# The FFN output projections as seven quarter products by tokens

## The chip, the cores and the metric

The kernel runs on one core of a Trainium2 chip. TensorE (PE) multiplies matrices, VectorE (DVE), ScalarE (ACT) and GpSimd (POOL) do elementwise work, and SyncE (SP) issues most transfers between HBM and the on-chip memory SBUF. PE's results land in PSUM, in eight banks of 128 partitions x 512 float32. Each engine works through its own instructions in order and waits for the others by semaphores. The metric is the device time of one execution in microseconds, as the median of several runs.

## The reference

A decoder trunk of two layers over 512 tokens and 1024 features, all in float32. Each layer has a token mixer (retention in layer 0, a gated linear recurrence, LRU, in layer 1) and a feed-forward network (FFN):

```python
def swiglu_ffn(x, w_in, w_out):
    gate, up = jnp.split(x @ w_in, 2, axis=-1)
    return (jax.nn.silu(gate) * up) @ w_out

# in the loop over the layers, behind the mixer:
    f = swiglu_ffn(rms_norm(x, norm_g[layer, 2]), ffn_w_in[layer], ffn_w_out[layer])
    x = x + rms_norm(f, norm_g[layer, 3])
```

The hidden width is 2816, which is 22 tiles of 128. The change concerns the last product, `h @ w_out` (512 x 2816 by 2816 x 1024), its norm over the 1024 features of each token, and the addition to `x`, once in each layer.

## The kernel before

**Precision.** A float32 value is split into a high part (`hi`, a cast to fp32r by ACT) and a low part (`lo`, the difference, by DVE), and a product is three matmuls (`mm3`, lines 289 to 291): high by high, high by low and low by high. So each weight chunk of 128 x 1024 costs one cast on ACT (L170) and one subtraction on DVE (L172) before PE can use it.

**Order.** One program writes all engines' instructions. A virtual clock, moved on by the columns of each matmul, decides what is written when: `later.after(ns, f)` puts `f` behind `ns` more of matmul time, `later.until` writes waiting work until something is there. Engines then follow that written order. Weight chunks are handled by `advance`: while one is used, the next ones are split up to `LEAD_S` = 12000 ns ahead, at most `HELD` = 8 at once, and their loads are issued ahead of that by SP. Memory for chunks, parts and intermediates comes from 50 slots of 128 x 1024.

**The FFN's input projection** already works by seven products of quarters in place of eight (a Strassen scheme in Winograd's form), pair of feature tiles by pair: products `p1` to `p7` with the weight forms `b11`, `t1`, `b21`, `t2`, `b22`, `t3`, `t4`, where `t1` to `t4` are sums of quarters made by accumulating loads (`Form.add`, L195, POOL's queue adds from HBM into the chunk). The activations are the stationary operand (128x128, loaded by LDWEIGHTS), the weight forms stream by 512 columns. There are five pairs per layer; `turn` (L999) transposes the gated result by four 128x128 transposes into one bank, and ACT copies it to the tiles `hf` of `h`, features on the partitions (L1000).

**The output projection** (`out_proj` with `quick=True`) is the plain product. Its stationary operand is the weight (`wh_fo`, `wl_fo`), and `h` streams: `halve` (L1145, L1146) splits `hf` into `hh` and `hl`. The 1024 features go in four groups of two tiles of 128, with 22 x 2 x 3 matmuls each: groups 0 to 2 with all 512 tokens (396 matmuls of 512 columns), the last one by two halves of 256 tokens (264 of 256). `tile_done` squares each tile (L616), scales it by the gain (L618) and adds the squares (L617); `finish` then sums the squares over the partitions by matmuls with ones (`st_`, L384), takes the root (`rchain`, L362 to L373), spreads it over partitions by two 128x128 matmuls (`rb_`, L398), multiplies (L624), adds the residual (L628, DVE and POOL) and stores (L629). In layer 0, `finish` of the second half lies in the LRU's first matmuls (`ps_u`, `ps_y`), and also writes the LRU's input tiles `Xl`; in layer 1 it is the end of the program.

Of the kernel before, what the change touches and what calls it, by code (L numbers as in the profile page):

```python
# [115 lines left out]
def trunk(ctx: ExitStack, tc: tile.TileContext, t: dict):  # L116
# [58 lines left out]
    class Form(Item):  # L175
# [326 lines left out]

    def product(key, r, banks, first, pre, done=None):

        for e in range(2):
            with Chunk("s", *key, WEIGHTS[r], e) as w:
                for p in range(2):
                    for i in range(2):
                        x = pre.left(LEFT[r], 2 * e + i, p)
                        mm3(banks[p], x, [z[:, i * S:(i + 1) * S] for z in w], first and not e + i, e + i == 2, True)  # L510
                    if e and done:
                        done(p)
# [86 lines left out]
    def out_proj(name, K, H, gi, x_src, pre, out, joined=1, halved=1, quick=False):  # L599
# [57 lines left out]
        for a, b in HALVES:  # L657
# [42 lines left out]
    def plan_ffn(layer):  # L700
# [287 lines left out]
    def ffn(layer, pre, x_src, nxt, out, mid=None):  # L988


        H, HF = [None] * KF, []
        A, B, C = ([acc(f"{z}{layer}_{p}") for p in range(2)] for z in "abc")
        def turn(hs, put):

            for m in range(hs[0].shape[-1] // 256):
# [43 lines left out]
        def closed(half):  # L1039
# [32 lines left out]
        def pair(j, r, to):  # L1072
# [4 lines left out]
            def gated():  # L1077
                hs, g = kept["u"], kept["g0"]
                for p in range(2):
                    dve.scalar_tensor_tensor(out=hs[p], in0=hs[p], scalar=pre.cols[p], in1=g[p], op0=ALU.mult, op1=ALU.mult)  # L1080
                later.after(W_TURN, lambda: turn(hs, lambda m: to[m][:, :, :256]))

# [33 lines left out]
            elif r == "p4":  # L1116
# [25 lines left out]

        def halve(n):
            f, hi, lo = HF[n], slot(f"hh{layer}_{n}", F32R), slot(f"hl{layer}_{n}", F32R)
            act.copy(hi, f)  # L1145
            dve.tensor_tensor(lo, f, hi.bitcast(F32), op=ALU.subtract)  # L1146
            for m in range(2):
                H[2 * n + m] = hi[:, m * S:(m + 1) * S], lo[:, m * S:(m + 1) * S]

# [4 lines left out]
        for j in range(PAIRS):  # L1154
            for r in LATER_PAIR if j else FIRST_PAIR[2:]:
# [223 lines left out]
```

## Time and profile before

| | us |
|---|---|
| median of 3 runs (lowest, highest) | 1355.41 (1354.25, 1356.55) |
| the profiled execution | 1356.11 |
| its span from first to last instruction | 1354.3 |
| PE busy | 1324.1 |
| PE's weight loads busy | 1122.6 |
| DVE busy | 826.6 |
| ACT busy | 712.3 |
| POOL busy | 135.7 |

The span begins at 0 in all rows. PE's busy time counts matmuls whose ends are modelled: a 512-wide one lasts 0.39 us in the rows, and the next one begins 0.23 us after it began, so lengths of a stretch are read from starts. The granted clock of PE was 0.996 of full speed over the span.

### The profile page before, as it was taken

What the parts mean: (1) busy time and instruction counts of PE and PEld (TensorE: products, weight loads), DVE (VectorE), ACT (ScalarE), POOL (GpSimd) and SP (SyncE); (2) the same over time, 40 slices, a digit from 0 to 9 for tenths busy, and PEclk for the clock granted to TensorE, in tenths of its full rate; (3) what the DMA queues carried; (4) which work ended last, traced back from release to release, by engine and by line L of the source; (5) the groups of instructions that cost most, each with busy time, mean ns of one, the idle gap of its engine ahead of it and who ended that gap; (6) DMA issues with size and microseconds to landing.
All of it is one profiled execution on the core that took longest, in us unless ns stands there. A gap on an engine that the chain in (4) does not pass through costs nothing.

```text
span 1354.3 us, 17267 instructions
## 1 busy us (share of the span) xinstructions
PE 1324.1 (98%) x6616; PEld 1122.6 (83%) x6616; DVE 826.6 (61%) x1285; ACT 712.3 (53%) x1063; POOL 135.7 (10%) x161
## 2 busy tenths in 40 slices
PE   7999999999999999999999999999999999999995
PEld 6888888887898878888889988888988888888895
DVE  7756665675359766566322887888489555584203
ACT  4645555476237665566322547687467556474211
POOL 1001010100010111110000800000011212100001
PEclk9999999999999999999999999999999999999998
DMA  8247567563476678784323542224576787753211
GB/s 323 63 106 176 142 168 184 141 186 110 125 185 181 190 175 183 190 187 140 103 84 109 167 146 78 78 94 156 156 205 185 174 214 176 169 161 110 69 63 63
DMA packets 65652, 200.26 MB, mean 148 GB/s; under 512 B 7104, under 2 KB 15424, under 8 KB 65568
## 3 DMA queue, kind: packets, MB, share of 16 engines
q1 hardware_dynamic: 48560, 140.40, 31.1%
q0 software_dynamic: 15856, 57.70, 23.3%
q8 instruction: 52, 0.85, 0.3%
q10 hardware_dynamic: 1152, 1.05, 0.2%
q14 instruction: 32, 0.26, 0.1%
HBM read 190.73 MB, written 8.39 MB: 147 GB/s over the span
## 4 chain that ended last, share of the span: by engine, by line
PE 91%; DVE 3%; ACT 2%; DMA 1%; issue 1%; POOL 1%; SPq 0%; POOLq 0%; DVEq 0%; ACTq 0%
PE ps_fo L289 6%; PE ps_fo L290 6%; PE ps_fo L291 6%; PE b L289 4%; PE b L291 4%; PE b L290 4%; PE c L289 4%; PE c L291 4%; PE c L290 4%; PE a L291 2%; PE a L290 2%; PE a L289 2%; PE ps_ro L290 2%; PE ps_ro L291 2%; PE ps_ro L289 2%; PE ps_y L289 1%
## 5 line engine op out<-in xcount | busy, mean ns | idle before, releaser
L289 PE MATMUL ps_fo<-hh,wh_fo 128*128 128x512 f32 (+1 forms) x440 | 153.2, 348 | 0.0
L291 PE MATMUL ps_fo<-hh,wl_fo 128*128 128x512 f32 (+1 forms) x440 | 152.5, 347 | 0.0
L290 PE MATMUL ps_fo<-hl,wh_fo 128*128 128x512 f32 (+1 forms) x440 | 152.5, 347 | 0.0
L195 POOL DMA_DIRECT2D wr<-in_w_s x84 | 71.7, 883 | 667.0 <-DVE wl_s_b L172 363.7
L172 DVE TENSOR_TENSOR wl_s_t<-wr,wh_s_t 128x1024 fp32r<-128x1024 f32 x80 | 95.6, 1221 | 35.2 <-ACT wh_s_t L170 35.1
L291 PEld LDWEIGHTS ps_fo<-hh,wl_fo 128*128 128x128 f32 x440 | 83.3, 189 | 10.4
L289 PEld LDWEIGHTS ps_fo<-hh,wh_fo 128*128 128x128 f32 x440 | 83.3, 189 | 10.2
L290 PEld LDWEIGHTS ps_fo<-hl,wh_fo 128*128 128x128 f32 x440 | 83.3, 189 | 10.1
L172 DVE TENSOR_TENSOR wl_s_b<-wr,wh_s_b 128x1024 fp32r<-128x1024 f32 x60 | 71.6, 1221 | 23.9 <-ACT wh_s_b L170 23.7
L170 ACT CAST wh_s_t<-wr 128x1024 fp32r<-128x1024 f32 x80 | 81.6, 1054 | 5.3 <-DMA wr<-in_w_s 5.3
L172 DVE TENSOR_TENSOR wl_fo<-wr,wh_fo 128x1024 fp32r<-128x1024 f32 (+1 forms) x48 | 51.8, 1130 | 17.6 <-ACT wh_fo L170 17.6
L170 ACT CAST wh_s_b<-wr 128x1024 fp32r<-128x1024 f32 x60 | 61.2, 1059 | 0.0
L172 DVE TENSOR_TENSOR wl_s_v_t<-wr,wh_s_v_t 128x1024 fp32r<-128x1024 f32 x24 | 29.4, 1223 | 30.1 <-ACT wh_s_v_t L170 29.9
L170 ACT CAST wh_fo<-wr 128x1024 fp32r<-128x1024 f32 (+1 forms) x48 | 44.0, 986 | 0.0
L195 POOL DMA_DIRECT2D wr<-in_w_vg x24 | 20.5, 932 | 223.0 <-DVE wl_s_v_t L172 128.9
L1000 ACT COPY hf<-turn 128x512 f32<-128x512 f32 x40 | 21.5, 589 | 32.2 <-PE turn L999 32.2
L1120 ACT ACTIVATE h<-b,y_pref 128x512 f32<-128x512 f32 x20 | 13.7, 690 | 44.0 <-PE b L291 44.0
L1125 DVE SCALAR_TENSOR_TENSOR h<-p,y_pref,h 128x512 f32<-128x512 f32 x20 | 14.9, 750 | 33.6 <-ACT h L1120 33.6
L170 ACT CAST wh_s_v_t<-wr 128x1024 fp32r<-128x1024 f32 x24 | 25.2, 1049 | 17.9 <-DMA wr<-in_w_vg 17.8
L289 PE MATMUL c<-wh_s_b,Xf_s4h 128*128 128x512 f32 x80 | 33.1, 414 | 0.0
L289 PE MATMUL b<-wh_s_t,Xf_11h 128*128 128x512 f32 x80 | 31.4, 392 | 0.0
L291 PE MATMUL c<-wh_s_b,Xf_s4l 128*128 128x512 f32 x80 | 31.3, 392 | 0.0
(1294 smaller groups left out, 3951.8 us busy)
## 6 DMA issues: line engine op xcount, KB each, us to landing
wr<-in_w_s POOLq DMA_DIRECT2D x84, 512.0 KB, 7.3
wr<-in_w_s SPq DMA_DIRECT2D x68, 512.0 KB, 5.9
wr<-in_w_fo SPq DMA_DIRECT2D x40, 512.0 KB, 3.7
wr<-in_w_vg SPq DMA_DIRECT2D x30, 512.0 KB, 3.7
wr<-in_w_vg POOLq DMA_DIRECT2D x24, 512.0 KB, 8.7
wr<-in_w_li SPq DMA_DIRECT2D x24, 512.0 KB, 4.0
wr<-in_w_ro SPq DMA_DIRECT2D x16, 512.0 KB, 4.3
wr<-in_w_lo SPq DMA_DIRECT2D x12, 512.0 KB, 3.9
```

Of the source, the lines that this page charges most:

```text
L170: act.copy(hi[:, :c], raw[:, :c])
L172: dve.tensor_tensor(lo[:, :c], raw[:, :c], hi[:, :c].bitcast(F32), op=ALU.subtract)
L195: pool.dma_start(self.source(), self.adds.pop(0), accum_op=ALU.add)
L289: pe.matmul(out, lhsT=lh, rhs=rh, start=bool(first), stop=False, skip_group_check=chained)
L290: pe.matmul(out, lhsT=lh, rhs=rl, start=False, stop=False, skip_group_check=chained)
L291: pe.matmul(out, lhsT=ll, rhs=rh, start=False, stop=bool(last), skip_group_check=chained)
L1000: act.copy(put(m), ps.rearrange("p (m t) -> p m t", m=2))
L1120: act.activation(g[p], B[p], AF.Silu, scale=pre.cols[2 + p])
L1125: dve.scalar_tensor_tensor(out=g[p], in0=hs[p], scalar=pre.cols[2 + p], in1=g[p], op0=ALU.mult, op1=ALU.mult)
```

## The change

The output projection of each FFN becomes seven quarter products as well, by tokens: `h` is taken as four quarters of 256 tokens x 1408 hidden features (11 tiles), the weight as four of 1408 x 512. The products come in the order `p1`, `p5`, `p2`, `p6`, `p3`, `p4`, `p7`, each with 11 x 2 x 3 matmuls of 512 columns, 462 per layer. Tokens are now on the partitions of the result: `h`'s forms are stationary, weight forms stream. The results gather in three pairs of banks `A`, `B`, `C`.

- `plan_fold` lists 42 weight chunks per layer (six of each form, the last of 512 columns): 24 loads by SP and 24 accumulating ones by POOL's queue. Before there were 24 chunks, loaded plainly.
- `Folded` makes `h`'s seven forms from the tiles `hf`: three quarters are split piece by piece (33 casts L735 and lows L738 of 128x256), four sums `s1`, `s2`, `s4`, `s3` are added by DVE (44 of 128x256, L729) and split by groups of four pieces (12 casts L707, lows L710). Before, `h` was split in 11 casts and lows of 128x1024.
- The sum of squares is now a row sum along the free dimension (ACT, `square`), the root a number per partition, and the scaled result is turned back by transposes (`add`, L846: four of 128x128 into one bank, eight such turns per layer). One DVE instruction (L848) then multiplies with the gain and adds the residual from PSUM, in place of L618, L624 and L628; the matmuls `st_` and `rb_` of this norm are gone.
- The first token half is finished under `p4` and `p7`, the second after `p7`: in layer 0 beside the LRU's first matmuls, in layer 1 as the end.

The core of the diff:

```diff
+        ORDER = ((0, 0), "s1", (0, 1), "s2", "s4", (1, 1), "s3")
...
+    FOLD = ("p1", "p5", "p2", "p6", "p3", "p4", "p7")
+    FOLD_SUMS = {"t1": ("b11", "b12"), "t2": ("t1", "b22"), "t3": ("", "b12", "b22"), "t4": ("t2", "b21")}
...
+    def fold_proj(name, H, gi, x_src, pre, out):
...
+        def after_p7(p):
+            dve.tensor_tensor(u[p], A[p], u[p], op=ALU.add)
+            dve.tensor_tensor(five[p], five[p], A[p], op=ALU.subtract)
+            square(1, 0, p, u[p])
+            square(1, 1, p, five[p])
...
+                        pt = aux(f"turn_f{name}_{h}{j}")
+                        for c in range(2):
+                            for p in range(2):
+                                pe.transpose(pt[:, c * 256 + p * P:][:, :P], cols[j // 4][p][:, (j + c) % 4 * P:][:, :P], ident)
+                            turned[j + c] = pt[:, c * 256:(c + 1) * 256]
+                    dve.scalar_tensor_tensor(out=yg[j][:, a:b], in0=turned[j], scalar=ng[:, gi, j:j + 1], in1=xs[j][:, a:b], op0=ALU.mult, op1=ALU.add)
+                    (act if pre is None and j % 2 else nc.sync).dma_start(out[j * P:(j + 1) * P, a:b], yg[j][:, a:b])
...
+        for n, (r, banks, first, done) in enumerate((("p1", A, True, after_p1), ("p5", C, True, after_p5), ("p2", A, False, after_p2),
+                                                     ("p6", B, False, after_p6), ("p3", C, False, None), ("p4", B, False, after_p4),
+                                                     ("p7", A, True, after_p7))):
+            H.allowed = n + 2
+            product((name,), r, banks, first, H, done, H.n)
...
-        plan_out(f"fo{layer}_", t["w_fo"][4 * layer:4 * layer + 4], KF)
+        plan_fold(f"fo{layer}", t["w_fo"][4 * layer:4 * layer + 4], KF // 2)
...
-        def last():
-            run(PAIRS - 1, "p4")
-            for n in range(2 * PAIRS - 1, 2 * PAIRS + 1):
-                later.after(W_LAST + 1500 * n - 13500, lambda n=n: halve(n))
-
-        later.after(W_P4, last)
-        out_proj(f"fo{layer}_", KF, H, 4 * layer + 3, x_src, nxt, out, quick=True)
+        later.after(W_P4, lambda: run(PAIRS - 1, "p4"))
+        fold_proj(f"fo{layer}", fold, 4 * layer + 3, x_src, nxt, out)
```

What stands where. Names are the program's with most numbers left out: `wl_s_fo_t_..` is the low part of a summed weight form, `Fs` a sum of `h` pieces, `Fp` a part of a form, `turn_ffo` a turn of the change, `Fu` and `F5` the two column halves of the result for the second token half.

VectorE in the middle of layer 1's output projection, before:

```order
L172 TENSOR_TENSOR wl_fo_1_16_10422<-wr_10302,wh_fo_1_16_10421 128x1024
L172 TENSOR_TENSOR wl_fo_1_20_10452<-wr_10332,wh_fo_1_20_10451 128x512
L172 TENSOR_TENSOR wl_fo_2_0_10482<-wr_10366,wh_fo_2_0_10481 128x1024
L172 TENSOR_TENSOR wl_fo_2_4_10512<-wr_10400,wh_fo_2_4_10511 128x1024
L172 TENSOR_TENSOR wl_fo_2_8_10542<-wr_10425,wh_fo_2_8_10541 128x1024
```

VectorE under the third product of layer 1's fold, with the change:

```order
L729 TENSOR_TENSOR Fsfo1s_1s<-hf_3_0_9609,Fsfo1s_1s 128x256
L181 TENSOR_TENSOR wl_s_fo_t_0_10638<-wr_9952,wh_s_fo_t_0_10637 128x1024
L729 TENSOR_TENSOR Fsfo1s_2s<-hf_3_1_9610,Fsfo1s_2s 128x256
L729 TENSOR_TENSOR Fsfo1s_2s<-hf_4_0_9901,Fsfo1s_2s 128x256
L710 TENSOR_TENSOR Fpfo1s_1l<-Fsfo1s_1s,Fpfo1s_1h 128x1024
L729 TENSOR_TENSOR Fsfo1s_2s<-hf_4_1_9902,Fsfo1s_2s 128x256
L181 TENSOR_TENSOR wl_s_fo_t_1_10663<-wr_9971,wh_s_fo_t_1_10662 128x1024
L710 TENSOR_TENSOR Fpfo1s_2l<-Fsfo1s_2s,Fpfo1s_2h 128x768
L181 TENSOR_TENSOR wl_s_fo_t_2_10684<-wr_10052,wh_s_fo_t_2_10683 128x1024
```

Where only weight lows stood, sums and lows of `h`'s forms now stand among more of them.

TensorE in the LRU's first matmuls behind layer 0's projection, at the second half's norm, before (`rb_postfo` spreads the root over the partitions):

```order
L289 MATMUL ps_u_0_6156<-Xl_3h,wh_u_0_5853 128x256
L290 MATMUL ps_u_0_6156<-Xl_3h,wh_u_0_5853 128x256
L291 MATMUL ps_u_0_6156<-Xl_3h,wl_u_0_5854 128x256
L398 MATMUL rb_postfo__256_6273<-dg_postfo__256_0_6235,ones_sq 128x128
L398 MATMUL rb_postfo__256_6273<-dg_postfo__256_1_6237,ones_sq 128x128
L289 MATMUL ps_u_1_6157<-Xl_3h,wh_u_0_5853 128x256
```

TensorE there with the change, 51 matmuls after the fold's last:

```order
L299 MATMUL ps_u_0_6250<-Xl_2h,wh_u_0_6209 128x256
L300 MATMUL ps_u_0_6250<-Xl_2h,wh_u_0_6209 128x256
L301 MATMUL ps_u_0_6250<-Xl_2h,wl_u_0_6210 128x256
L846 MATMUL turn_ffo_10_6319<-ident,Fufo_0_5210 128x128 x4
L299 MATMUL ps_u_1_6251<-Xl_2h,wh_u_0_6209 128x256
L300 MATMUL ps_u_1_6251<-Xl_2h,wh_u_0_6209 128x256
```

The turn takes the place of the norm's own matmuls; three more turns follow further on.

VectorE at the same place with the change, from the root to the turned result:

```order
L383 SCALAR_TENSOR_TENSOR y_foldfo_1_6237<-tm_foldfo_1_6239,y_foldfo_1_6237 128x2
L181 TENSOR_TENSOR wl_u_4_6259<-wr_6132,wh_u_4_6258 128x1024
L181 TENSOR_TENSOR wl_y_4_6277<-wr_6170,wh_y_4_6276 128x1024
L827 TENSOR_SCALAR Fufo_0_5210<-Fufo_0_5210,y_foldfo_1_6237 128x512 x2
L848 SCALAR_TENSOR_TENSOR yfo_0_5199<-turn_ffo_10_6319,ng,xrfo_0_5903 128x256 x2
```

Two weight lows of the LRU stand between the root and the scale that the turn needs; before, the root went to `dg_postfo` and PE directly.

## Rows read from the trace of the kernel before

**Rows 1.** The page: engines' busy time and share, and the chain that ended last.

```profile
PE 1324.1 (98%) x6616; PEld 1122.6 (83%) x6616; DVE 826.6 (61%) x1285; ACT 712.3 (53%) x1063; POOL 135.7 (10%) x161
PE 91%; DVE 3%; ACT 2%; DMA 1%; issue 1%; POOL 1%; SPq 0%; POOLq 0%; DVEq 0%; ACTq 0%
```

**Rows 2.** PE's waits, layer 0's projection and after: us in total, times, longest.

```profile
PE rb_postfo__256_6273 L398 <- DVE dg_postfo__256_0_6235 L391: 1.3, 1, 1.3
```

**Rows 3.** Stretches: length, busy us (instructions) by engine, PE clock, DMA share, GB/s.

```profile
1128.50:1168.50 40.00, 40.00 (x186) 33.10 (x185) 22.20 (x22) 21.42 (x28) 6.82 (x8) 1.00 0.79 185
1190.00:1209.00 19.00, 19.00 (x89) 15.79 (x88) 17.30 (x17) 13.57 (x17) 0.00 (x0) 1.00 0.52 142
1230.00:1260.00 30.00, 30.00 (x135) 24.82 (x134) 12.21 (x12) 10.43 (x14) 0.00 (x0) 1.00 0.39 114
```

**Rows 4.** PE's instructions in time: start us, duration, engine, line, operation.

```profile
622.97 0.48 PE L289 MATMUL ps_fo<-hh,wh_fo 128*128 128x512 f32 x1
...
751.71 0.28 PE L289 MATMUL ps_u<-Xl_0h,wh_u 128*128 128x256 f32 x1
...
1128.33 1.03 PE L999 MATMUL turn<-ident,u 128*128 128x128 f32 x8
1129.12 0.48 PE L289 MATMUL a<-wh_s_b,Xf_00h 128*128 128x512 f32 x1
...
1168.33 1.03 PE L999 MATMUL turn<-ident,u 128*128 128x128 f32 x8
...
1208.78 0.60 PE L999 MATMUL turn<-ident,u 128*128 128x128 f32 x4
1209.13 0.48 PE L289 MATMUL ps_fo<-hh,wh_fo 128*128 128x512 f32 x1
1209.44 0.40 PE L290 MATMUL ps_fo<-hl,wh_fo 128*128 128x512 f32 x1
```

**Rows 5.** PE in time, end of layer 1's projection.

```profile
1337.63 0.28 PE L290 MATMUL ps_fo<-hl,wh_fo 128*128 128x256 f32 x1
1337.75 0.28 PE L291 MATMUL ps_fo<-hh,wl_fo 128*128 128x256 f32 x1
```

**Rows 6.** DVE in time, end of layer 1's input projection.

```profile
1192.13 1.22 DVE L172 TENSOR_TENSOR wl_s_b<-wr,wh_s_b 128x1024 fp32r<-128x1024 f32 x1
1193.27 1.22 DVE L172 TENSOR_TENSOR wl_s_t<-wr,wh_s_t 128x1024 fp32r<-128x1024 f32 x1
...
1196.91 0.69 DVE L1075 TENSOR_TENSOR u<-c,u 128x512 f32<-128x512 f32 x1 [0.16 <-ACT u L1106]
```

**Rows 7.** All engines in time, the tail behind the last matmul.

```profile
1339.67 0.26 ACT L362 ACTIVATE tm_postfo__256_11109<-st_postfo__256_11103,eps 128x2 f32<-128x2 f32 x1 [0.86 <-PE st_postfo__256_11103 L384]
...
1340.82 0.29 DVE L391 TENSOR_SCALAR dg_postfo__256_0_11116<-ident,y_postfo__256_11107 128x128 f32<-128x128 f32 x1
...
1344.07 0.41 DVE L628 TENSOR_TENSOR yfo__2_10156<-yfo__2_10156,xrfo__2_10910 128x256 f32<-128x256 f32 x1
...
1344.40 0.41 DVE L624 TENSOR_TENSOR yfo__4_10157<-yfo__4_10157,rb_postfo__256_11120 128x256 f32<-128x256 f32 x1
...
1345.84 0.50 DVE L628 TENSOR_TENSOR yfo__6_10158<-yfo__6_10158,xrfo__6_10914 128x256 f32<-128x256 f32 x1
```

**Rows 8.** Groups: busy us, mean ns | idle before, releaser; page, then 1170 to 1338.

```profile
L172 DVE TENSOR_TENSOR wl_fo<-wr,wh_fo 128x1024 fp32r<-128x1024 f32 (+1 forms) x48 | 51.8, 1130 | 17.6 <-ACT wh_fo L170 17.6
L170 ACT CAST wh_fo<-wr 128x1024 fp32r<-128x1024 f32 x20 | 20.2, 1057 | 0.0
L170 ACT CAST wh_fo<-wr 128x512 fp32r<-128x512 f32 x4 | 2.5, 629 | 0.0
```

**Rows 9.** DMA queues 1128.5 to 1168.5 (packets, MB, share); page: us to landing.

```profile
q0 software_dynamic: 1155, 4.20, 57.7%
q1 hardware_dynamic: 868, 3.16, 20.9%
wr<-in_w_s POOLq DMA_DIRECT2D x84, 512.0 KB, 7.3
```

More of the change, by code (lines that the diff above doesn't have):

```diff
@@ L158, in trunk @@
         early = False
+        most = HELD
         def source(self):
@@ L501, in left, with product @@
             return [z[:, i * 256 + p * P:][:, :P] for z in self.forms[q]]
-    def product(key, r, banks, first, pre, done=None):
-        for e in range(2):
-            with Chunk("s", *key, WEIGHTS[r], e) as w:
+    def product(key, r, banks, first, pre, done=None, n=4):
+        for e in range(0, n, 2):
+            with Chunk("s", *key, WEIGHTS[r], e // 2) as w:
                 for p in range(2):
[L508 to L511, printed above, removed]
+                    for i in range(min(2, n - e)):
+                        x = pre.left(LEFT[r], e + i, p)
+                        mm3(banks[p], x, [z[:, i * S:(i + 1) * S] for z in w], first and not e + i, e + i == n - 1, True)
+                    if e + 2 >= n and done:
                         done(p)
@@ L666, in out_proj, with __init__, src, where @@
             finish(a, b)
+    class Folded:
+        ORDER = ((0, 0), "s1", (0, 1), "s2", "s4", (1, 1), "s3")
+        NEEDS = {"s1": (1,), "s2": (0, 1), "s4": (0, 1), "s3": (0, 1)}
+        def __init__(self, name, n, raw, there):
+            self.name, self.n, self.raw, self.there = name, n, raw, there
+            self.parts, self.sums, self.got = {}, {}, set()
+            self.allowed = 2
+            by = {z[0]: z for z in Corners.SUMS}
+            self.todo = []
+            for k, f in enumerate(self.ORDER):
+                self.todo += [(k, f, by.get(f), m) for m in range(n)]
+        def src(self, q, m):
+            return self.raw(2 * m + q[1])[:, q[0] * 256:(q[0] + 1) * 256]
+        def where(self, store, f, m, kind, dt):
+            if (f, m // 4) not in store:
+                store[f, m // 4] = [slot(f"{kind}{self.name}{f}_{m // 4}{z}".replace("(", "").replace(")", "").replace(", ", ""), dt) for z in ("hl" if dt == F32R else "s")]
+            return [z[:, m % 4 * 256:][:, :256] for z in store[f, m // 4]]
+        def group(self, f, m):
+            g, c = m // 4, (m % 4 + 1) * 256
+            src = self.sums[f, g][0]
+            self.where(self.parts, f, m, "Fp", F32R)
+            hi, lo = self.parts[f, g]
+            act.copy(hi[:, :c], src[:, :c])
+            def low():
+                dve.tensor_tensor(lo[:, :c], src[:, :c], hi[:, :c].bitcast(F32), op=ALU.subtract)
+                self.got |= {(f, z) for z in range(4 * g, m + 1)}
+            later.after(1000, low)
+        def pump(self):
+            if not self.todo:
+                return
+            ready = (z for z in self.todo if z[0] <= self.allowed and all(self.there(z[3], h) for h in self.NEEDS.get(z[1], (z[1][0],))))
+            z = next(ready, None)
+            if not z:
+                later.after(300, self.pump)
+                return
+            self.todo.remove(z)
+            _, f, total, m = z
+            if total:
+                _, x, y, op = total
+                x, y = (self.src(z, m) if isinstance(z, tuple) else self.where(self.sums, z, m, "Fs", F32)[0] for z in (x, y))
+                dve.tensor_tensor(self.where(self.sums, f, m, "Fs", F32)[0], x, y, op=op)
+                if m % 4 == 3 or m == self.n - 1:
+                    later.after(W_GROUP, lambda: self.group(f, m))
+            else:
+                hi, lo = self.where(self.parts, f, m, "Fp", F32R)
+                src = self.src(f, m)
+                act.copy(hi, src)
+                def low():
+                    dve.tensor_tensor(lo, src, hi.bitcast(F32), op=ALU.subtract)
+                    self.got.add((f, m))
+                later.after(600, low)
+            later.after(W_PUMP, self.pump)
+        def left(self, f, m, p):
+            later.until(lambda: (f, m) in self.got)
+            return [z[:, m % 4 * 256 + p * P:][:, :P] for z in self.parts[f, m // 4]]
@@ new lines, in trunk, with plan_fold @@
+    FOLD = ("p1", "p5", "p2", "p6", "p3", "p4", "p7")
+    FOLD_SUMS = {"t1": ("b11", "b12"), "t2": ("t1", "b22"), "t3": ("", "b12", "b22"), "t4": ("t2", "b21")}
+    def plan_fold(name, src, n):
+        forms = {}
+        for r in FOLD:
+            f = WEIGHTS[r]
+            for e in range((n + 1) // 2):
+                base, *adds = FOLD_SUMS.get(f, ("", f))
+                quarters = [src[QUARTERS.index(q)][:, 1024 * e:min(1024 * (e + 1), 512 * n)] for q in adds]
+                first = None if base else quarters.pop(0)
+                forms[f, e] = Form(("s", name, f, e), forms[base, e] if base else None, first, quarters)
+                forms[f, e].most = HELD_F
@@ L1000, in turn @@
                 act.copy(put(m), ps.rearrange("p (m t) -> p m t", m=2))
+                here.add((base + m, half))
         def tiles(j):
@@ L1049, in gated @@
                     dve.scalar_tensor_tensor(out=hs[p][:, :256], in0=hs[p][:, 256:], scalar=y, in1=hs[p][:, :256], op0=ALU.mult, op1=ALU.mult)
-                later.after(W_TURN_R, lambda: turn([h[:, :256] for h in hs], lambda m: rest_to[m][:, :, half * 256:(half + 1) * 256]))
+                later.after(W_TURN_R, lambda: turn([h[:, :256] for h in hs], lambda m: rest_to[m][:, :, half * 256:(half + 1) * 256], 0, half))
             def when():
@@ L1141, in run @@
             later.after(300, lambda: pair(j, r, to[j]))
[L1143 to L1148, printed above, removed]
+        here = set()
+        fold = Folded(f"fo{layer}", KF // 2, lambda j: HF[j // 2][:, j % 2 * S:][:, :S], lambda m, h: (m, h) in here)
         opening()
```

103 lines of the change are left out of this document (93 added, 10 removed).

## The prediction

> **What bounds the kernel now.** I read the page's first lines, then who TensorE (PE) waited for, then busy time by stretch, and last single instructions around the two places that the change touches. PE is busy 98% of the span and makes 91% of the chain of work that ended last [rows 1]; in the two output projections it waits for nothing but 1.3 us at one matmul of the norm in layer 0 [rows 2]. So a PE instruction that goes takes its time with it as long as what feeds PE stays ahead. In the second layer's output projection VectorE (DVE) is busy 12.21 of 30 us, and the DMA engines 0.39 of theirs [rows 3]: there is slack there, and the change spends it.
>
> **What PE no longer does.** In layer 1 the projection runs from the first `ps_fo` matmul at 1209.13 to the end of the last at 1337.75 + 0.28 [rows 4, 5]; since a 256-wide matmul is followed by the next after 0.12, that is 128.74 us up to where a next one would have started. In layer 0 it is the same 128.74, from 622.97 to the first `ps_u` matmul at 751.71 [rows 4]. Inside lie the last product of the FFN's input projection, 24 matmuls, and its turn, 8 transposes, which both kernels have. A pair of FFN products, 168 matmuls of 512 and two turns of 8, takes 40.00 us from one turn (1128.33) to the same one of the next pair (1168.33); a turn holds PE 0.79 to the next matmul, whose own successor comes 0.31 later and not 0.23, so it costs 0.87, and a matmul (40.00 − 1.74)/168 = 0.2277 [rows 4]. Thus the projection proper is 128.74 − 24 × 0.2277 − 0.87 = 122.4 us in each layer.
>
> **What PE does instead.** Seven products of 11 k-tiles × 2 banks × 3 matmuls, 462 of 512 columns. That is the shape, the operand order (activations 128x128 loaded as weights, 512 columns of weight form streaming) and the helper of the FFN pairs, so 0.2277 holds: 105.2 us, which is 2.75 pairs. A turn of 4 holds PE from 1208.78 to 1209.13 with the same late successor, 0.44 in all [rows 4]. Layer 1 has four such turns beside products (the other four are in the tail): 107.0 us against 122.4, **15.4 gained**. Layer 0 has all eight beside other matmuls, 105.2 + 3.5 = 108.7. There the norm by rows also goes from PE: a sum over partitions and a pair of 128x128 matmuls, which I price like a turn of 4, 0.4 each, and the 1.3 wait [rows 2]; before is 122.4 + 2.1 = 124.5. A new wait takes that one's place: the turn of half 1 stands behind 51 LRU matmuls of 256 columns, 51 × 0.12 = 6.1 us after the last product, while its columns need sums, squares, root and scale, 5.0 us after the last matmul by the tail's working below, and two weight lows of 1.14 stand between root and scale on DVE [rows 6]: ready at about 7.8, so PE waits 1.7, and I add 0.4 for a PSUM bank. Bounds 0 and 5. Layer 0: 110.8 against 124.5, **13.7 gained**.
>
> **The tail.** Before, the last matmul ends at 1338.03, the last DVE addition at 1345.84 + 0.50 = 1346.34, and the span (the table above) at 1354.3: 8.31 us of arithmetic, then 7.96 from there to the end, a store's issue and landing [rows 7]. After, counted from the last matmul's end: four 128x512 operations out of PSUM at 0.69, one and a half of them ahead of it, to 1.8; ACT's square at 0.63, what a 128x512 cast takes, to 2.4; sum and root as before, from 1339.67 to 1340.82, to 3.8; two scales of 128x512 to 5.0; a turn to 5.6; eight 128x256 operations at 0.41 to 8.9 [rows 6 to 8]. The same 7.96 behind it, as the stores are the same eight of 128 KB on the same two queues. The residual addition, which POOL shared, is now part of the eight. So **0.6 lost**; bounds 0 lost (operations follow each other faster than they last, 0.33 for 0.41 [rows 7]) and 2 lost.
>
> **What hides the rest.** Per layer DVE gets 35 weight lows of 128x1024 and 7 of 512, 44 sums and 33 lows of 128x256, 8 group lows of 1024 and 4 of 768, eight 512-wide steps and a half's finish. Back to back a 1024 low takes 1.14 (starts at 1192.13 and 1193.27), a 256 one 0.33 [rows 6, 7]; with 0.60 for 512: 35 × 1.14 + 7 × 0.60 + 77 × 0.33 + 8 × 1.14 + 4 × 0.87 + 8 × 0.60 + 6 = 93 us in 105. ACT has the matching casts, under 1.06 for each 1024 and 0.63 for the others [rows 8], some 80 us. DVE has been seen busy 17.30 of 19 us while PE did not stop [rows 3], so 0.89 of the time can be kept up. The tightest stretch is under the third product, `p2`: 11 sums and 3 group lows of `s4`, the six lows of `t2` and the first of quarter (1,1): about 14.7 us in a product's 15.0. A low of a summed weight form now also waits for its addition by DMA, and behind it in DVE's order stand the sums of the next h form, for which PE waits in the end. The weights are split some four chunks, 10 us, before PE wants them, and that is the cover: a DVE delay below that costs nothing, one above it all of it.
>
> DMA: a layer's weights come as 22 loads' worth of 512 KB and 22 accumulating ones, 11.5 MB each, beside 2.1 MB of residual and 1 MB of stores. In an FFN pair the software queue (the accumulating loads) moves 4.20 MB in 57.7% of 16 engines' 40 us, 88 engine-us per MB; the hardware queue 3.16 MB in 20.9%, 42 per MB [rows 9]. The fold then needs (11.5 × 88 + 14.6 × 42)/16 = 102 of 105 us, against 0.79 of the time in a pair with PE never stopping [rows 3]. That is the least comfortable ratio of all. Two things speak against a stall: additions are issued once the form before is split, a product or more ahead of use, and one lands in 7.3 us [rows 9], so landing can double unseen; and packet time is not yet a queue, since loads begin under the last FFN pair and DMA has nothing else to do. The Trainium skill (SBUF — State Buffer, section "SBUF: two separate sides") puts what 16 DMA engines bring into SBUF at about 436 GB/s; by that figure the 26 MB would be an estimated 60 us, and this resource no question. The pair's rows say otherwise, 185 GB/s at a share of 0.79, so the trace's ratio is the one I keep.
>
> **The sum.** 13.7 + 15.4 − 0.6 = 28.5 us. The profiled execution took 1356.11, its span 1354.3; it lies 0.70 above the median. 1356.11 − 28.5 = 1327.6, and by the median **1327**. PE's terms are sure within 1; the LRU wait and the tail leave 1324 to 1331.
>
> **Rivals.** (a) *DVE's order costs what its instructions last, not what they step by.* With 1.22, 0.69, 0.41 as durations the same list is 104 us, and if each of the 42 weight lows waits for ACT's cast as now (17.6 us for 48, 0.37 each [rows 8]), 120. Less the 10 of cover, that is 110 against 105: 4 to 5 lost per layer, 1336. For it: the lists under `p2` have no slack. Against: rows step at 1.14, and the waits of now fall where DVE is idle anyway.
> (b) *DMA is the bound.* If packets under a load of 0.97 take a fifth longer than in the pair, 122 − 10 = 112: 7 lost per layer, 1341. For it: the share; against: the lead.
> (c) **Slower than before:** *each ACT to DVE hand-over waits.* The 45 new casts and lows of h forms would wait 0.37 too, 17 us more, 136 per layer; 136 − 10 = 126, 21 lost per layer, 1369. It decides from DVE time per layer above 105 + 10 + 14 = 129 us on. For it: one engine order holds three chains, weights, h forms, norm; against: the order puts sums between cast and low.
> (d) *It does not do what it says:* 462 matmuls that step slower than 0.2277, for a stationary operand that changes each time. The FFN pairs change theirs as often, so hardly.
>
> **Chances.** Forecast 0.74, (a) 0.12, (b) 0.08, (c) 0.05, rest 0.01. The range reaches to (a) and (b): 1323 to 1342. A change below 0.2%, 2.7 us, about what a measurement can tell here, needs 13 lost per layer, between (b) and (c): faster 0.93, same 0.02, slower 0.05.
>
> **What would show it.** Right: 924 matmuls out of `a`, `b`, `c` for the folds at 0.228, a projection of some 105 us per layer, PE's waits in it under 5 us, a wait of about 2 at the LRU's first turn of half 1, DVE busy over 0.85, the end some 17 us after the last matmul. Wrong: PE waiting for lows of `t2` or of `s4` in the second to fourth product (a, c), or DVE lows waiting for DMA with landing times far above 7.3 (b).

## The result and the profile after

The changed kernel takes 1325.05 us (median of 4 runs, 1323.96 to 1326.96) against 1355.33 for the kernel before: a ratio of 0.9778, 95% interval 0.9761 to 0.9795, 30.3 us gained. The forecast was 1327 and faster. Its profiled execution took 1323.96 us with a span of 1321.8, so the two spans that are compared here differ by 32.5; the rest is one execution against a median.

On the page of the changed kernel (engines' busy time; the software queue of the accumulating loads; the folds' accumulating loads with KB and us to landing) PE has lost 28 us of busy time against [rows 1], DVE has gained 91, ACT 59, and the software queue went from 57.70 to 80.77 MB:

```profile
PE 1296.0 (98%) x6252; PEld 1087.5 (82%) x6252; DVE 917.2 (69%) x1487; ACT 771.4 (58%) x1181; POOL 154.8 (12%) x185
q0 software_dynamic: 22768, 80.77, 33.2%
wr<-in_w_fo POOLq DMA_DIRECT2D x40, 512.0 KB, 9.3
```

Where the time went, by starts of single instructions. PE in the changed kernel (start, duration, operation; in brackets the idle time before and who ended it):

```profile
621.71 0.48 PE L299 MATMUL afo<-wh_s_fo_b,Fpfo_0h 128*128 128x512 f32 x1
623.08 0.50 PE L300 MATMUL afo<-wl_s_fo_b,Fpfo_0h 128*128 128x512 f32 x1 [0.90 <-DVE wl_s_fo_b L181]
...
735.97 0.28 PE L299 MATMUL ps_u<-Xl_0h,wh_u 128*128 128x256 f32 x1
...
737.97 0.36 PE L299 MATMUL ps_u<-Xl_0h,wh_u 128*128 128x256 f32 x1 [0.41 <-DVE F5fo L813]
...
744.34 0.85 PE L846 MATMUL turn_ffo<-ident,Fufo 128*128 128x128 f32 x4 [0.69 <-DVE Fufo L827]
...
1194.62 0.48 PE L299 MATMUL afo<-wh_s_fo_b,Fpfo_0h 128*128 128x512 f32 x1
1196.01 0.50 PE L300 MATMUL afo<-wl_s_fo_b,Fpfo_0h 128*128 128x512 f32 x1 [0.90 <-DVE wl_s_fo_b L181]
...
1308.68 0.39 PE L301 MATMUL afo<-wh_s_fo_t,Fpfo1s_2l 128*128 128x512 f32 x1
```

| stretch | before | after | difference |
|---|---|---|---|
| start to layer 0's first projection matmul | 622.97 | 621.71 | -1.26 |
| layer 0's projection, to the first `ps_u` | 128.74 | 114.26 | -14.48 |
| from there to layer 1's first projection matmul | 457.42 | 458.65 | +1.23 |
| layer 1's projection, to the last matmul's end | 128.90 | 114.45 | -14.45 |
| last matmul's end to the last DVE instruction's end | 8.31 | 9.80 | +1.49 |
| from there to the span's end | 7.96 | 2.93 | -5.03 |

The column of before comes from [rows 4, 5, 7]; the differences add up to 32.5. The first row lies ahead of any change. That place came at 620.77 to 623.31 in the kernels below that leave everything ahead of it as it was, so it is the start of one execution. The last row was in nobody's sum.

PE's waits in the changed kernel (us in total, times, longest) are the start of the program, the turns (4.7 of the 5.4 in the tail), and 0.9 at each layer's first weight low; those left out lie in parts that the change leaves alone:

```profile
PE ps_v L299 <- ACT Xr_0h L427: 6.3, 1, 6.3
PE turn_ffo L846 <- DVE Fufo L827: 5.4, 2, 4.7
...
PE afo L300 <- DVE wl_s_fo_b L181: 1.8, 2, 0.9
...
PE ps_u L299 <- DVE F5fo L813: 0.9, 2, 0.5
```

In the stretches that answer to [rows 3] (length, busy us by engine, PE's clock, DMA share, GB/s), in layer 1, PE never stops, DVE goes to 14.62 of 15 us and the DMA engines' share to 1.07:

```profile
1210.00:1226.00 16.00, 16.00 (x76) 13.36 (x75) 11.18 (x17) 8.96 (x12) 5.11 (x6) 1.00 1.07 220
...
1241.00:1256.00 15.00, 15.00 (x67) 12.40 (x67) 13.89 (x23) 12.73 (x25) 5.11 (x6) 1.00 0.76 135
...
1271.00:1286.00 15.00, 15.00 (x68) 12.44 (x67) 14.62 (x33) 9.14 (x14) 0.26 (x1) 1.00 1.04 291
```

So three questions are left: whether each layer gives what its stretch says, what ended the program 5 us earlier, and how far the two nearly full resources, DVE and DMA, are from costing something.

### The profile page after: what moved, and what is told of

It reads as the page before. It is cut to its first block, busy times and chain, and to the rows that moved or that the text cites. A ratio compares the mean times of both kernels' runs of the same rounds, so it can differ in the third digit from the quotient of the medians.

```text
span 1321.8 us, 17030 instructions
## 1 busy us (share of the span) xinstructions
PE 1296.0 (98%) x6252; PEld 1087.5 (82%) x6252; DVE 917.2 (69%) x1487; ACT 771.4 (58%) x1181; POOL 154.8 (12%) x185
## 3 DMA queue, kind: packets, MB, share of 16 engines
q0 software_dynamic: 22768, 80.77, 33.2%
## 4 chain that ended last, share of the span: by engine, by line
PE 90%; DVE 3%; ACT 3%; issue 2%; DMA 1%; SPq 0%; POOL 0%; DVEq 0%; ACTq 0%; POOLq 0%
PE b L299 4%; PE b L301 4%; PE b L300 4%; PE c L299 4%; PE c L301 4%; PE c L300 4%; PE a L300 2%; PE a L299 2%; PE ps_ro L300 2%; PE a L301 2%; PE ps_ro L301 2%; PE ps_ro L299 2%; PE afo L300 2%; PE afo L301 2%; PE afo L299 2%
## 5 line engine op out<-in xcount | busy, mean ns | idle before, releaser
L181 DVE TENSOR_TENSOR wl_s_t<-wr,wh_s_t 128x1024 fp32r<-128x1024 f32 x80 | 95.8, 1222 | 41.3 <-ACT wh_s_t L179 41.3
L181 DVE TENSOR_TENSOR wl_s_b<-wr,wh_s_b 128x1024 fp32r<-128x1024 f32 x60 | 71.6, 1221 | 25.1 <-ACT wh_s_b L179 24.9
L181 DVE TENSOR_TENSOR wl_s_fo_t<-wr,wh_s_fo_t 128x1024 fp32r<-128x1024 f32 (+1 forms) x48 | 54.1, 1138 | 15.8 <-ACT wh_s_fo_t L179 15.7
L205 POOL DMA_DIRECT2D wr<-in_w_fo x48 | 41.0, 869 | 192.8 <-DVE wl_s_fo_t L181 95.5
L181 DVE TENSOR_TENSOR wl_s_fo_b<-wr,wh_s_fo_b 128x1024 fp32r<-128x1024 f32 (+1 forms) x36 | 40.5, 1132 | 14.2 <-ACT wh_s_fo_b L179 14.1
L181 DVE TENSOR_TENSOR wl_s_v_t<-wr,wh_s_v_t 128x1024 fp32r<-128x1024 f32 x24 | 29.4, 1223 | 29.9 <-ACT wh_s_v_t L179 27.5
L179 ACT CAST wh_s_fo_t<-wr 128x1024 fp32r<-128x1024 f32 (+1 forms) x48 | 45.9, 976 | 6.0 <-DVE yfo L848 4.5
L205 POOL DMA_DIRECT2D wr<-in_w_vg x24 | 20.5, 931 | 222.4 <-DVE wl_s_v_t L181 127.8
L179 ACT CAST wh_s_fo_b<-wr 128x1024 fp32r<-128x1024 f32 (+1 forms) x36 | 34.6, 979 | 3.4 <-PE bfo L300 2.0
L179 ACT CAST wh_s_v_t<-wr 128x1024 fp32r<-128x1024 f32 x24 | 25.1, 1048 | 17.7 <-DMA wr<-in_w_vg 17.6
L1105 ACT COPY hr<-turn_r 128x512 f32<-128x512 f32 x16 | 9.4, 586 | 38.9 <-PE turn_r L1103 38.9
L299 PE MATMUL b<-wh_s_t,Xf_s2h 128*128 128x512 f32 x80 | 31.3, 391 | 0.0
L300 PE MATMUL c<-wl_s_b,Xf_s4h 128*128 128x512 f32 x80 | 31.3, 391 | 0.0
L299 PE MATMUL c<-wh_s_t,Xf_s1h 128*128 128x512 f32 x80 | 31.3, 391 | 0.0
```

Of the source, the lines that this page charges most:

```text
L179: act.copy(hi[:, :c], raw[:, :c])
L181: dve.tensor_tensor(lo[:, :c], raw[:, :c], hi[:, :c].bitcast(F32), op=ALU.subtract)
L205: pool.dma_start(self.source()[:, :self.cols], self.adds.pop(0), accum_op=ALU.add)
L299: pe.matmul(out, lhsT=lh, rhs=rh, start=bool(first), stop=False, skip_group_check=chained)
L300: pe.matmul(out, lhsT=lh, rhs=rl, start=False, stop=False, skip_group_check=chained)
L1105: act.copy(hr, pt)
```

## One layer at a time

`l0_only` changes layer 0's projection alone, `l1_only` layer 1's; the other stays as `out_proj` with `halve`.

```diff
-        plan_fold(f"fo{layer}", ...)
+        if layer in (0,):      # (1,) in l1_only
+            plan_fold(f"fo{layer}", ...)
+        else:
+            plan_out(f"fo{layer}_", ...)
```

> Only layer 0's projection is seven products, layer 1's is as before. Theory (the gain is PE time that goes, layer by layer): the two traces have layer 0's projection at 128.74 us before and 114.26 after, and the LRU with the rest up to layer 1's projection 1.23 us longer, so 13.3 us gained: about 1342. Rival (the folds lean on each other, or the gain sits in the end of the program): under 10 us gained, over 1345. The end behind the last matmul stays at some 16.3 us, as layer 1 is that of before.

> Only layer 1's projection is seven products, layer 0's is as before. By the two traces layer 1's projection gives 14.45 us and the end behind the last matmul 3.54 (16.27 to 12.73), together 18.0: about 1337. Rival (the 5.0 us of the end in which no instruction and no transfer is seen, 7.96 against 2.93 after the last DVE instruction, is chance of one execution): 13.0 gained, about 1342.

`l0_only` took 1336.82 us against 1355.83 (ratio 0.9867, 0.9852 to 0.9883), `l1_only` 1338.20 (0.9873, 0.9857 to 0.9890). The stretches repeat: layer 0's projection 621.85 to 736.11, 114.26 us, in `l0_only`, and 128.74 in `l1_only`. `l1_only` is near what was expected. `l0_only` gained 19.0 and not 13.3, and the place where the surplus sits is the end, where nothing was changed: the same four POOL and four DVE additions as before, with the span's end at 1335.2.

```profile
1331.00 0.84 POOL L638 TENSOR_TENSOR yfo__6_10218<-yfo__6_10218,xrfo__6_10975 128x256 f32<-128x256 f32 x1 [0.16 <-DVE yfo__6_10218 L634]
...
1331.62 0.50 DVE L638 TENSOR_TENSOR yfo__6_10218<-yfo__6_10218,xrfo__6_10975 128x256 f32<-128x256 f32 x1
...
1332.15 0.33 SPq L639 DMA_DIRECT2D out_x<-yfo__6_10218  x1
```

The quiet stretch, from the end of the last DVE instruction (here 1332.12) to the span's end, is 3.08 here and 7.96 in the kernel before. One of the four executions of `l0_only` took 1340.88 us, 4 more than the other three; whether the long end came back in it was not traced. Each layer alone loses that stretch, and both together lose it once: 19.0 + 17.6 - 5.0 = 31.6, about the 30.3 of the whole change.

## What ends the program

In the kernel before, the last store lands some 1.8 us after its issue at 1346.37, and then the trace shows no instruction and no transfer for 6 us (the last two columns are DMA share and GB/s):

```profile
1348.00:1350.00 2.00, 0.00 (x0) 0.00 (x0) 0.00 (x0) 0.00 (x0) 0.00 (x0) 0.50 0.00 0
...
1352.00:1354.30 2.30, 0.00 (x0) 0.00 (x0) 0.00 (x0) 0.00 (x0) 0.00 (x0) 0.50 0.00 0
```

POOL works in that tail (four additions) and not in the changed one. `before_nopool` gives those additions to DVE:

```diff
-                        eng = dve if isinstance(pre, Corners) else pool if pre is not None or j % 2 else dve
+                        eng = dve if isinstance(pre, Corners) or pre is None else pool
```

> The kernel before, with the four residual additions in each of layer 1's two halves that POOL made put on DVE (L628). Theory P (the end waits for POOL, whose last instruction lies 8.2 us ahead of the span's end in the trace of before and 20 us ahead in that of after): the quiet stretch after the last DVE instruction falls from 7.96 to about 3, DVE's row of additions grows by 4 x 0.33 = 1.3, and the time goes to about 1351.7. Rival (the quiet stretch has nothing to do with POOL): 7.96 stays, about 1356.6.

It took 1351.30 us (0.9968, 0.9955 to 0.9981). Its last DVE instructions in time, with the span's end at 1348.6:

```profile
1344.83 0.75 DVE L628 TENSOR_TENSOR yfo__6_10158<-yfo__6_10158,xrfo__6_10914 128x256 f32<-128x256 f32 x2
```

From 1345.58 to 1348.6 it is 3.02. So 4.5 us were to be had in the old kernel by one word. `after_pool` does the opposite, one POOL addition at the end of the changed kernel:

```diff
+                    if pre is None and h and j == 5:
+                        pool.tensor_tensor(yg[0][:, :256], xs[j][:, a:b], yg[j][:, a:b], op=ALU.add)
```

> The changed kernel with one POOL addition of 128x256 more, of data that nobody reads, behind the sixth of the eight last tiles. Theory P (the end waits for POOL): POOL's last instruction ends about 1 us before DVE's, the span's end lies some 8 us behind POOL's, and the time grows by 4 to 5 us, to about 1329.5. Rival: no change, 1325.

1327.30 us: 2.2 more than the changed kernel, and a quiet stretch of 5.32 behind POOL's last instruction (1325.8 the span's end), not 8. The intervals of the two ratios overlap (0.9777 to 0.9806 here, 0.9761 to 0.9795 for the changed kernel), so the 2.4 us more at the end rests on the traces:

```profile
1318.74 1.73 DVE L848 SCALAR_TENSOR_TENSOR yfo<-turn_ffo,ng,xrfo 128x256 f32<-128x256 f32 x4 [0.42 <-PE turn_ffo L846]
1319.76 0.72 POOL L851 TENSOR_TENSOR yfo<-xrfo,yfo 128x256 f32<-128x256 f32 x1 [28.17 <-DVE yfo L848]
```

With POOL in the tail the stretch is thus 7.96, 5.3 or 3.1, without it 2.8 to 3.0. The next idea was that the place in POOL's instruction stream decides. Two kernels put eight small instructions on POOL ahead of layer 0's FFN, in the kernel before and in `after_pool`:

```diff
+        if not layer:
+            for i in range(8):
+                pool.memset(sp.tile([P, 4], F32, tag="spare", name=f"spare{i}", bufs=1), 0.0)
```

> The kernel before with eight small POOL memsets of an unused tile ahead of layer 0's FFN, nothing else. With POOL in the tail, the quiet stretch behind the last DVE instruction was 7.96 us in the kernel before (161 POOL instructions) and 3.08 in the kernel with layer 0 alone changed (169, and the very same tail); without POOL in the tail it is 2.9 to 3.0 in all. Theory Q (where POOL stands in its instruction stream at the end decides, nothing that it computes): with 169 the stretch is 3 again, the time about 1351. Rival (the stretch comes from layer 0's projection being the plain one): 7.96, about 1355.5.

> The kernel after_pool, in which the quiet stretch was 5.33 us, with the same eight memsets ahead of layer 0's FFN. Theory Q: the stretch changes by over 1 us one way or the other, and the time with it (1324 to 1330). Rival (POOL at the very end simply costs 2.4 us): 5.3 and 1327.3 stay.

That theory fell. `before_shift` took 1355.08 (0.9991, 0.9981 to 1.0), its quiet stretch is 7.60 (1345.50 to 1353.1); `after_pool_shift` 1327.73, with 5.24. Shown is: POOL in the last microseconds can lengthen the end, by 2.4 us in one kernel and by 5 in another, and without POOL there it was 3 in every kernel tried. What sets the amount, and why `l0_only` has POOL in the tail and yet 3.1, stays open.

## How much room DVE has

`dve44` writes each weight low of the folds twice (35 of 1024 and 7 of 512 columns per layer); `dve14` adds a piece of 256 columns instead.

```diff
             dve.tensor_tensor(lo[:, :c], raw[:, :c], hi[:, :c].bitcast(F32), op=ALU.subtract)
+            if self.key[1] in ("fo0", "fo1"):
+                m = c                       # 256 in dve14
+                dve.tensor_tensor(lo[:, :m], raw[:, :m], hi[:, :m].bitcast(F32), op=ALU.subtract)
```

> The changed kernel with each of the 84 weight lows of the folds (L181) written twice by DVE: 35 x 1.14 + 7 x 0.60 = 44 us more of DVE per layer. Theory (DVE has what is left of PE's 107 us per layer after 87 busy, and a cover of some 10 us, and no more): 87 + 44 - 107 - 10 = 14 lost per layer, about 1353, with PE waiting for L181's lows in the second to sixth product. Rival (DVE's own order already costs the cover, nothing is left over): over 24 lost per layer, over 1373. Rival (weights are far enough ahead that DVE hardly matters): under 5 per layer, under 1335.

> The changed kernel with 84 DVE instructions of 128x256 more, one behind each weight low of the folds: 42 x 0.33 = 14 us per layer. With 44 more, DVE was busy 139.5 of a fold's 150.1 us in layer 0, 0.93, where it is 93.6 of 114.3 in the changed kernel. Theory (DVE is the next bound, full at 0.93): (93.6 + 14)/0.93 = 115.7, so 1 to 2 lost per layer, 1327 to 1329. Rival (the order has no room: what is added costs the same from the first on): 35.9/44 x 14 = 11 lost per layer, 1347.

`dve44` took 1396.39 us (1.0303, 1.0272 to 1.0335): 71 more than the changed kernel, 36 per layer for 44 of DVE. `dve14` took 1344.82 (0.9918, 0.9898 to 0.9939): 20 more, 10 per layer for 14. Layer 0's projection as one stretch (columns as in [rows 3]), in the changed kernel:

```profile
621.70:736.00 114.30, 113.40 (x514) 93.73 (x513) 93.61 (x154) 73.97 (x117) 26.89 (x31) 1.00 0.91 229
```

In `dve44`, one of ten stretches from 622.3 to 772.4, and their sum:

```profile
682.00:697.00 15.00, 11.77 (x41) 8.69 (x42) 14.86 (x19) 10.23 (x20) 2.56 (x3) 0.89 0.47 77
...
sum 150.10, PE 127.79 PEld 98.41 DVE 139.48 ACT 73.49 POOL 26.56; mean PE 12.78 PEld 9.84 DVE 13.95 ACT 7.35 POOL 2.66
```

In `dve14`, the sum of eight stretches from 622 to 747:

```profile
sum 125.00, PE 117.32 PEld 95.16 DVE 110.72 ACT 73.92 POOL 26.56; mean PE 14.67 PEld 11.89 DVE 13.84 ACT 9.24 POOL 3.32
```

And who PE waited for there most (us in total, times, longest):

```profile
PE turn_ffo L848 <- DVE yfo L850: 3.6, 1, 3.6
PE afo L302 <- DVE wl_s_fo_b L183: 2.0, 2, 1.4
```

Whom DVE itself waited for, in layer 0's projection of the changed kernel:

```profile
DVE wl_s_fo_t L181 <- ACT wh_s_fo_t L179: 7.1, 7, 1.8
DVE wl_s_fo_b L181 <- ACT wh_s_fo_b L179: 7.0, 5, 3.2
```

DVE is busy 93.6 of 114.3 us in the changed kernel, yet 14 more cost 10. The 20 us in which it stands are not free: it waits there for ACT's casts (14 us in layer 0 at L181) and cannot do what is queued behind. Of what was added, 4 us (`dve14`) to 8 (`dve44`) found room per layer, and those waits at L181 shrank to 10.5 and 8.0; in `dve44` DVE is busy for 0.93 of the stretch and is plainly the bound. In five of its ten stretches PE is granted 0.78 to 0.93 of its clock, beside waits, and PE's busy time grows from 113.4 to 127.8 us; that is part of the loss. For `dve44` the theory of 14 lost per layer fell, and the rival of over 24 held. The expectation that took 0.93 as the point from which DVE counts was wrong for `dve14`, the other one (0.8 us for each us added, from the first on) right within 1 us per layer.

## How much room DMA has

`no_adds` leaves the accumulating loads of the folds out; `dma_more` adds for each weight chunk of the folds a 256 KB transfer within HBM.

```diff
# no_adds, in Form.add
+                if self.most == HELD_F and self.key[1] in ("fo0", "fo1"):
+                    self.adds.pop(0)
+                    continue
# dma_more, in Form.split
+            if self.key[1] in ("fo0", "fo1"):
+                l, e = int(self.key[1][2]), len(junked)
+                nc.sync.dma_start(t["junk"][e], t["w_fo"][4 * l + e % 4][:, e // 4 % 10 * 512:][:, :512])
+                junked.append(e)
```

> The changed kernel without the 24 accumulating loads of each fold, so that the summed weight forms t1 to t4 are wrong. Theory (PE is the bound, DMA at a share near 1 is not waited for): PE's only wait inside the products is 0.9 us at the first weight low of each layer, and that one is for DVE behind ACT; the time stays within 1.5 us of the changed kernel's 1325. Rival (DMA is the bound of the stretches with a share of 1.03 to 1.07, hidden in waits put down to others): 5 us or more gained, 1320 or below.

> The changed kernel with a transfer of 256 KB between two places in HBM by SP's queue for each of the 84 weight chunks of the folds, read by nobody. At the pair's 42 engine-us per MB that is 10.5 MB and at least 28 us of 16 engines per layer, beside about 102. Theory (DMA is covered by loads that run ahead, but is the next bound): 102 + 28 = 130 against 107 and a lead of some 15, so up to 8 lost per layer: 1325 to 1341. Rival (DMA has nothing left): 20 or more lost per layer, over 1365. Rival (share is no measure of the bound at all): 1325, landing times unchanged.

Without the additions: 1324.34 us (0.9761, 0.9737 to 0.9786), 0.7 less than the changed kernel's 1325.05 and inside its runs. The plain loads then land in 4.1 us and not 5.8, and PE's wait of 0.9 at each first low is still there:

```profile
wr<-in_w_fo SPq DMA_DIRECT2D x40, 512.0 KB, 4.1
...
PE afo L303 <- DVE wl_s_fo_b L181: 1.8, 2, 0.9
```

So the additions cost PE nothing that could be measured, though the DMA share goes to 1.07 with them. With the extra transfers: 1344.65 us (0.9913, 0.9891 to 0.9935), 20 more, 10 per layer, which is over the theory's 8 and half of the rival's 20. From 640 to 740 (share of 16 engines in tenths, GB/s in 40 slices, then issues with KB and us to landing) the engines never rest:

```profile
DMA  9999999999999999899999999999999999999999
GB/s 266 267 260 246 250 244 242 243 247 315 407 419 409 412 404 252 170 193 257 239 228 224 247 351 420 410 312 250 252 238 248 306 408 401 411 401 363 231 236 319
...
wr<-in_w_fo POOLq DMA_DIRECT2D x14, 512.0 KB, 10.8
wr<-in_w_fo SPq DMA_DIRECT2D x11, 512.0 KB, 9.7
xrfo<-x SPq DMA_DIRECT2D x4, 512.0 KB, 17.9
```

So the ratio that the prediction took from the FFN pair, 102 us of 16 engines in 105, was near the truth (0.91 of layer 0's 114.3 us in the changed kernel is 104): there was room for the change and for not much more. Where no additions are under way the slices reach 400 to 420 GB/s, the transfers within HBM included; in the changed kernel, which has none of those, it is 397 from 1264 to 1267. Where additions are under way the slices of `dma_more` show 170 to 270. The figure of some 436 GB/s that the Trainium skill (SBUF — State Buffer, section "SBUF: two separate sides") gives for what 16 engines bring into SBUF lies a little above the first and says nothing of the second.

## The waits that were left, and a faster version

The first weight low of a fold is late for a reason that the rows show. ACT ahead of layer 1's first product in the changed kernel:

```profile
1190.26 1.05 ACT L707 CAST Fpfo1s_1h<-Fsfo1s_1s 128x1024 fp32r<-128x1024 f32 x1 [2.48 <-DVE Fsfo1s_1s L729]
...
1192.96 1.06 ACT L179 CAST wh_s_fo_b<-wr 128x1024 fp32r<-128x1024 f32 x1
```

DVE at the same place:

```profile
1193.26 1.22 DVE L710 TENSOR_TENSOR Fpfo1s_1l<-Fsfo1s_1s,Fpfo1s_1h 128x1024 fp32r<-128x1024 f32 x1
1194.40 0.42 DVE L738 TENSOR_TENSOR Fpfo_0l<-hf_-1_0_8456,Fpfo_0h 128x256 fp32r<-128x256 f32 x1
1194.73 1.22 DVE L181 TENSOR_TENSOR wl_s_fo_b<-wr,wh_s_fo_b 128x1024 fp32r<-128x1024 f32 x1
```

ACT stands 2.48 us before the cast of a group of `s1`, which PE needs 15 us later, and the weight's cast that PE needs next is queued behind it; on DVE the group's low stands ahead of the weight's. `tuned` writes such casts later, the second half's scale earlier, and keeps PE going through the tail:

```diff
-W_F1 = 2500
-W_F2 = 3000
-W_GROUP = 1200
+W_F1 = 800
+W_F2 = 4700
+W_GROUP = 2500
...
+        if pre is None:
+            for i in range(19):
+                z = H.parts["s3", 0]
+                pe.matmul(B[0], lhsT=z[0][:, :P], rhs=z[0][:, :512], start=i == 0, stop=i == 19 - 1, skip_group_check=True)
```

> The changed kernel with three waits taken away: the cast of a group of h sums is written 2500 instead of 1200 ns after its last sum (W_GROUP), so that ACT doesn't stand 2.5 us behind DVE just ahead of the first weight cast; the scale of the second half is written 800 instead of 2500 ns after the root (W_F1, and W_F2 4700 for 3000), ahead of one of the two LRU lows; and 19 matmuls that nobody reads keep PE going in layer 1 between the last product and the turns, where the granted clock is 0.5 of full. By the rows: the wait of 0.9 with its gap, 1.1 in each layer, goes, 0.6 at the LRU's first turn, and 1 us of the end, as 8 turns take 2.06 and 8 of full clock 1.03: 3.8 in all, 1321. Rival (what stands later in DVE's order then comes too late): the waits return at the second or third product, 1325.

1319.99 us (0.9735, 0.9714 to 0.9755), 5.1 less than the changed kernel, whose interval it lies below. PE at layer 1's start, then the tail of `tuned`, with one row of a stretch (columns as in [rows 3]):

```profile
1193.10 0.48 PE L299 MATMUL afo<-wh_s_fo_b,Fpfo_0h 128*128 128x512 f32 x1
1193.42 0.40 PE L300 MATMUL afo<-wl_s_fo_b,Fpfo_0h 128*128 128x512 f32 x1
...
1306.16 4.47 PE L877 MATMUL bfo<-Fpfo1s_0h 128*128 128x512 f32 x19
...
1306.30:1311.00 4.70, 4.33 (x20) 3.27 (x19) 3.47 (x12) 3.43 (x10) 0.00 (x0) 1.00 0.00 0
...
1311.01 1.29 PE L846 MATMUL turn_ffo<-ident,Fufo 128*128 128x128 f32 x8 [0.38 <-DVE Fufo L827]
1311.90 3.35 DVE L848 SCALAR_TENSOR_TENSOR yfo<-turn_ffo,ng,xrfo 128x256 f32<-128x256 f32 x8 [0.64 <-PE turn_ffo L846]
```

The second matmul follows the first by 0.32 and not by 1.39, in both layers: the projections take 113.06 (622.52 to 735.58) and 113.22 us, 1.2 less each. The LRU's first turn no longer waits, and the stretch from layer 0's projection to layer 1's falls from 458.65 to 457.52. In the tail PE's clock is 1.00 until the turns, and the first two turns (eight transposes) take 1.29 us, where they took 2.06 at a granted clock of 0.50 after 4.7 us without work; DVE's eight instructions then follow without a gap, and the tail behind the last matmul is 11.88 us and not 12.73. That is 4.4 in these stretches; the other 0.7 of the 5.1 lies in none of them.

## Why the prediction was right, and where not

By stretch the change gave 13.3 us in layer 0, 14.5 in layer 1 and lost 1.5 in the tail, where the sum had 13.7, 15.4 and 0.6: 26.2 for 28.5. The 5.0 at the end of the program come on top.

**PE's terms held.** 462 matmuls at 0.2277 and four turns give 107.0 us; measured are 114.26 - 5.46 - 0.87 = 107.9 in layer 0 and as much in layer 1. The 0.9 over is the wait at the first weight low, 1.1 by starts, which the prediction didn't see (without it, in `tuned`, it is 106.7): it looked for late lows under the second to fourth product, where DVE is fullest, and not at the first, where ACT stands.

**Layer 0's end.** The stretch behind layer 0's projection grew by 1.23; the sum had four turns (1.76) and 2.1 of waits against 2.1 removed, so 1.8. The turn waited 0.7 by the profile, 0.85 by starts, not 1.7: it came 8.2 us after the last matmul's end (736.13 to 744.34), near the 7.8 forecast, but PE itself reached it later than at 6.1, since two bank waits, 1.2 us by starts where the sum had 0.4, had held it before.

**The tail's arithmetic** was put 0.6 longer and came out 1.5 longer, 9.80 for 8.31, inside its bound of 2. ACT squares four tiles one after the other, and the prediction counted the last alone, but that is 0.3 (2.7 us after the last matmul and not 2.4). It was made good, as the first transpose needs one scale and not two: it began at 4.68 and not 5.0. The 0.9 over the forecast of 8.9 come mostly from the turns, which ran at the granted clock of 0.50: the first one kept DVE waiting for 1.25 and not 0.6, and DVE's row of eight took 3.87 and not 3.3, 0.42 of it a wait for the next turns:

```profile
1309.21 0.63 ACT L781 ACTIVATE fqfo<-Fufo 128x512 f32<-128x512 f32 x1 [7.25 <-DVE Fufo L812]
...
1311.07 0.61 ACT L781 ACTIVATE fqfo<-F5fo 128x512 f32<-128x512 f32 x1
1311.59 0.19 ACT L781 ACTIVATION_READ_ACCUMULATOR fqfo<-F5fo 128x1 f32 x1
...
1313.75 2.06 PE L846 MATMUL turn_ffo<-ident,Fufo 128*128 128x128 f32 x8 [4.68 <-DVE Fufo L827]
...
1315.00 1.73 DVE L848 SCALAR_TENSOR_TENSOR yfo<-turn_ffo,ng,xrfo 128x256 f32<-128x256 f32 x4 [1.00 <-PE turn_ffo L846]
...
1317.14 1.73 DVE L848 SCALAR_TENSOR_TENSOR yfo<-turn_ffo,ng,xrfo 128x256 f32<-128x256 f32 x4 [0.42 <-PE turn_ffo L846]
...
1313.70:1318.00 4.30, 4.00 (x16) 2.97 (x16) 2.89 (x8) 0.81 (x2) 0.00 (x0) 0.50 0.36 120
```

**The end of the program** was the step that failed: "The same 7.96 behind it". It was 2.93. That POOL's additions have to do with it is shown by `before_nopool` (7.96 to 3.02); by what means, and why `l0_only` has them and 3.08, stays open. The 5 us went the right way and brought the time from what the other changed stretches would give, 1355.3 - 26.2 = 1329, to 1325; the forecast of 1327 lies between the two, as much by luck as by its sum, since 2.3 too much in one place stood against 5.0 too little in another. The trace of the kernel before had the cue: a store of 128 KB that lands in 1.8 us doesn't explain 7.96.

**The cover.** DVE's list of 93 us came out at 93.6 in layer 0's stretch, 0.82 of it and not the 0.85 that was to be a sign of being right. But the cover of 10 us, below which a DVE delay "costs nothing", was wrong. (The 0.89 of the time that the prediction holds possible is 17.30 of 19 us, so 0.91, and comes from a stretch with other chains in DVE's order.) `dve14` shows that 14 us more cost 10 per layer, so rival (a) stood much nearer than its 0.12 said: the 15 us of waits for ACT that it feared are there (14 in layer 0), though its longer durations are not. By these numbers they cost nothing as 93.6 + 14 = 107.7 is still 6.6 under the stretch's 114.3, and 4 to 8 is what the added work found. Rival (b) was as near: 10 per layer lost with two fifths more bytes, though its own condition, packets that take a fifth longer, did not show (104 us for the 102 forecast). Rivals (c) and (d) did not show.

## What to carry to other kernels

On this kernel, whose PE is full, counting matmuls at the step of like matmuls gave the new projection within 1 us in 107, as what feeds PE still fitted; whether it fits was not shown by DVE's idle time, most of which was waits that more work didn't fill. An in-order engine's busy time plus its waits for others is the better thing to compare with PE's time; here that left 6.6 us, and 4 to 8 were found. Follow the end of a program to its last microsecond: what is still running, on which engine, and what the last store explains. And keep late conversions for later products from standing, in an engine's order, ahead of the one that PE needs next.

## What was not expected of the hardware

- With POOL's elementwise work in the last microseconds the span ended 5.2 to 8.0 us after the last DVE instruction in four of five kernels (3.1 in the fifth), and 2.8 to 3.0 in all without it.
- The DMA engines' share can stand at 1.03 to 1.07 for 15 us at a time with no PE wait; the folds' accumulating loads landed in 9.3 us, those of the FFN pairs in 7.4.
- After 4.7 us without work PE was granted 0.50 of its clock, the lower of its two levels, for all 16 of the tail's transposes; 19 matmuls that nobody reads, put into that time, kept it at 1.00 up to the turns.
